# Attention as one written order over 40 units, with copies moved between ScalarE, VectorE and GpSimd

## The chip, the cores and the metric

The kernel runs on one core of a Trainium2 chip. The core has five engines that work side by side, each through its own instructions in order: TensorE (PE in the profile, matmuls, with PEld for its weight loads), VectorE (DVE), ScalarE (ACT), GpSimd (POOL) and SyncE (SP), which here issues nearly all DMA transfers. SBUF is the on-chip memory that all engines read; PSUM holds eight banks into which TensorE writes. The metric is the time of one execution on the device in microseconds (us); before the change it is 1604.54, the median of three runs (1601.63 to 1610.67).

## What is computed

A decoder block over 1024 tokens of width 1024, in float32. After a norm, one projection gives the inputs of two branches and of two gates: a state-space branch (branch a), and an attention branch with 8 heads of width 64 (branch b). The gated branches are merged, a feed-forward layer follows. The change concerns the attention:

```python
def one_block(args):
    qb, t0 = args
    z = jnp.einsum('bhqd,bhkd->bhqk', qb, kh) * scale
    q_pos = t0 + jnp.arange(Q_BLOCK, dtype=jnp.int32)[:, None]
    mask = key_pos < q_pos
    log_not = jnp.where(mask, jax.nn.log_sigmoid(-z), 0.0)
    suffix = lax.cumsum(log_not, axis=3, reverse=True) - log_not
    weights = jnp.where(mask, jnp.exp(jax.nn.log_sigmoid(z) + suffix), 0.0)
    return jnp.einsum('bhqk,bhkd->bhqd', weights, vh)
```

For every query a weight on each earlier key is needed, and it depends on a running sum over all keys between that key and the query. So the sums of one block of keys are carried on to the next block, from late keys to early ones.

## The kernel before

Heads are taken in four pairs (hp), the 1024 queries in two halves of 512 (Q). A pair and a half form a group. Within a group the keys are walked from late to early in blocks of 128 (kb). One step of this walk is a unit: two small blocks at once in the first step of a group, one block in the others. A group with Q=0 has three units, one with Q=1 has seven, so there are ten units per pair of heads and 40 in all. A unit covers 512 queries for two heads (tiles of 128 x 2 x 512) in 24 of the 40, and 384 in the 16 that lie on the diagonal and are cut by the mask.

A unit has three parts.

- `scores` (from L681): TensorE multiplies keys and queries into `z` in PSUM (L694). `z` is copied to SBUF as `wa`, with the mask added on the diagonal (L702, VectorE) or without (L704, VectorE). ScalarE computes abs, exp and log into `ws` (L705 to L707), VectorE completes the logarithm (L708). For the running sum in high precision, `ws` is split into a high part `wh` (L709, a cast on ScalarE) and the rest `wl` (L710, VectorE).
- the sums (L727 to L748): TensorE multiplies both parts by a triangle of ones into `acc` in PSUM (L731, L734), of which there is one buffer of two banks (the pool `accp`). Row 0 of it, added to the row so far, is the sum over all later keys (L740, L742, VectorE). It is written to DRAM (`cD`, L744) and read back spread over all 128 partitions as `wb` (L746), both issued by SP. The next unit subtracts that `wb` from its `wa` on GpSimd (L727) and its own `acc` on VectorE (L748). ScalarE takes the exponential (L749).
- the values (L753): TensorE multiplies the weights in `wa` by V into one PSUM bank per group, which ScalarE copies out at the group's end (L754).

Beside this runs work that does not depend on the attention and fills TensorE. It is 14 projection jobs: the queries and keys of head pairs 1 to 3 (`qk_proj`, six jobs) and the eight blocks of the second gate (`gate` with g=1). A job loads one weight block of 512 KB, splits it into a high and a low part (L411 on ScalarE or L413 on GpSimd, L414), and then issues two halves of 24 matmuls (L610) of 128 x 512 each. A half writes one PSUM bank, which is copied out by ScalarE (L647, L662) or VectorE (L645, L664). The pool for it, `mm`, has a single bank here, since the eight banks are shared out as one for `mm`, one for the values, four for `z` (two buffers) and two for `acc`. A gate block is then stored to DRAM (`gD`).

The order is not written by hand. A planner that simulates the kernel in time while it is built lays out each engine's instructions, first the ready ones, by their place in the program. The kernel influences it by edges that only order: `first=` in `qk_proj` and `gate` puts a weight load behind a chosen score matmul (`self.marks`, with `QPIN` and `PINS`). Behind the attention follows `branch_b`, which multiplies the outputs by w_b (L882) and applies the gates from DRAM.

Of the kernel before, what the change touches and what calls it, by code (L numbers as in the profile page):

```python
# [333 lines left out]
P = 128  # L334
KT = 8
# [37 lines left out]
class Turns:  # L373
# [5 lines left out]
    def tile(self, shape, dtype, name=None):  # L379
        pool, tag, *bufs = self.pools[self.n % len(self.pools)]  # L380
        self.n += 1
        return pool.tile(shape, dtype, name=tag, bufs=bufs[0] if bufs else None)


class Block:
# [295 lines left out]
    def scores(self, q, k, Q, kbs, work):  # L681


        nc = self.nc
        a, s = (work.tile([P, 2, 512], F32, name=t, bufs=b) for t, b in (("wa", WAB2), ("ws", WSB)))
        hi, lo = (work.tile([P, 2, 512], F32R, name=t, bufs=WHB) for t in ("wh", "wl"))
        z = self.zp.tile([P, 2, 512], F32, name="z")
        segs, f, prev, diag = [], 0, None, kbs[0] >= 4 * Q
        for kb in kbs:
            c = max(kb - 4 * Q, 0) * P  # L690
            w = 512 - c
            for x in range(2):
                h = slice(64 * x, 64 * x + 64)
                prev = nc.tensor.matmul(z[:, x, f:f + w], lhsT=k[h, P * kb:P * kb + P], rhs=q[h, 512 * Q + c:512 * Q + 512],  # L694
                                        start=True, stop=True)
            segs.append((kb, slice(f, f + w), slice(c, 512)))
            f += w
        self.marks.append(prev)
        at, st, ht, lt, z = (t[:, :, 0:f] for t in (a, s, hi, lo, z))
        if diag:  # L700
            m = P * (2 - len(kbs))
            nc.vector.tensor_tensor(at, z, self.mask[:, m:m + f].unsqueeze(1).broadcast_to([P, 2, f]), ALU.add)  # L702
        else:
            nc.vector.tensor_copy(at, z)  # L704
        nc.scalar.activation(st, at if diag else z, AF.Abs)  # L705
        nc.scalar.activation(st, st, AF.Exp, scale=-1.0)
        nc.scalar.activation(st, st, AF.Ln, bias=1.0)  # L707
        nc.vector.scalar_tensor_tensor(st, at, 0.0, st, ALU.max, ALU.add)  # L708
        nc.scalar.copy(ht, st)  # L709
        nc.vector.tensor_tensor(lt, st, ht.bitcast(F32), ALU.subtract)  # L710
        return a, (hi, lo), segs, f

    def heads(self, hp, q, k, V, work, out):


        nc = self.nc
        for Q in range(2):
            kbs = [(4 * Q + 3, 4 * Q + 2), (4 * Q + 1,), (4 * Q,)] + [(kb,) for kb in reversed(range(4 * Q))]
            av = self.avp.tile([P, 512], F32, name="mm")
            row = behind = None  # L720
            for unit in kbs:
                a, parts, segs, f = self.scores(q, k, Q, unit, work)
                kb, fs, c = segs[-1]
                if behind is not None:
                    old = slice(c.start + P if kb >= 4 * Q else 0, 512)
                    o = slice(old.start - c.start, 512 - c.start)
                    nc.gpsimd.tensor_tensor(a[:, :, o], a[:, :, o], behind[:, :, old], ALU.subtract)  # L727
                r = self.accp.tile([P, 2, 512], F32, name="acc")
                for x in range(2):
                    for n in range(2):  # L730
                        nc.tensor.matmul(r[:, x, 0:f], lhsT=self.upto, rhs=parts[n][:, x, 0:f], start=n == 0, stop=n == 1 and behind is not None)  # L731
                    if behind is None:
                        for n in range(2):
                            nc.tensor.matmul(r[:, x, f - P:f], lhsT=self.ones_r, rhs=parts[n][:, x, 0:P], start=False, stop=n == 1)  # L734
                if kb:
                    past, row = row, work.tile([P, 2, 512], F32, name="row", bufs=RWB)[0:1]
                    if c.start:
                        nc.gpsimd.memset(row[:, :, 0:c.start], 0.0)
                    if past is None:
                        nc.vector.tensor_copy(row[:, :, c], r[0:1, :, fs])  # L740
                    else:
                        nc.vector.tensor_tensor(row[:, :, c], past[:, :, c], r[0:1, :, fs], ALU.add)  # L742
                    d = self.cD[hp, Q, kb:kb + 1]
                    nc.sync.dma_start(out=d, in_=row.rearrange("p a b -> p (a b)"))  # L744
                    behind = work.tile([P, 2, 512], F32, name="wb", bufs=CBB)
                    nc.sync.dma_start(out=behind.rearrange("p a b -> p (a b)"), in_=d[0].partition_broadcast(P))  # L746
                for x in range(2):
                    nc.vector.tensor_tensor(a[:, x, 0:f], a[:, x, 0:f], r[:, x, 0:f], ALU.subtract)  # L748
                self.last_exp = nc.scalar.activation(a[:, :, 0:f], a[:, :, 0:f], AF.Exp)  # L749
                for kb, fs, c in segs:  # L750
                    for x in range(2):
                        h = slice(64 * x, 64 * x + 64)
                        nc.tensor.matmul(av[h, c], lhsT=V[:, kb, h], rhs=a[:, x, fs], start=kb == 4 * Q + 3, stop=kb == 0, skip_group_check=True)  # L753
            nc.scalar.copy(out[:, 512 * Q:512 * Q + 512], av)  # L754


    def ada_rest(self, ap, first):
# [423 lines left out]
    def run(self):  # L1181
        tc, nc, i = self.tc, self.nc, self.i
        with ExitStack() as es:
# [14 lines left out]
            w = (wp, "wh", "wl", wp, "ws", 2)  # L1198
# [3 lines left out]
            with ExitStack() as s1:  # L1202
                mm = s1.enter_context(self.pool("mm", 1, PSUM))
# [4 lines left out]
                gp = gps.enter_context(self.pool("g", GB, side="right"))  # L1208
# [12 lines left out]
                with ExitStack() as s3:  # L1221
                    with self.pool("ta", 2, side="right") as tp, \
# [12 lines left out]
                    vp = s3.enter_context(self.pool("v", 2))  # L1235
                    op = s3.enter_context(self.pool("o", 4))
                    with self.pool("tri", 1) as tri, self.pool("work", 1) as work, self.pool("zp", ZPB, PSUM) as self.zp, self.pool("acc", 1, PSUM) as self.accp:
                        self.avp = mg_
                        self.triangles(tri)
                        self.marks = []  # L1240
                        self.mm = mm
                        ops = []
                        for hp in range(4):
                            V = vp.tile([P, KT, P], F32, name="V")
                            nc.sync.dma_start(out=V, in_=self.vD.rearrange("(t p) d -> p t d", p=P)[:, :, P * hp:P * hp + P])
                            if hp:
                                qk.append(self.qk_proj(hp, qp, kp, self.marks[QPIN]))
                            q, k = qk[hp]
                            ops.append(op.tile([P, 1024], F32, name="o"))
                            self.heads(hp, q, k, V, work, ops[hp])  # L1250
# [4 lines left out]
                        for m in range(KT):  # L1255
                            self.gate(1, m, gp, self.marks[PINS[m]] if m else None, self.wring[2])
# [10 lines left out]
            with ExitStack() as s4:  # L1267
# [4 lines left out]
                wb = (self.W, "wb", "wb", wp, "ws", 2)  # L1272
# [43 lines left out]
```

## Time and profile before

| what | value |
|---|---|
| median of the runs | 1604.54 us |
| profiled execution, its own time | 1602.23 us |
| span of the profiled execution | 1600.5 us |
| busy: TensorE, VectorE, GpSimd, ScalarE | 1437.2, 1143.1, 783.8, 632.5 us |
| first score matmul to last value matmul | 409.4 to 728.5 us into the span |

A profile is one execution. Its time is a little longer than its span, from the first instruction to the last. Sums over parts of the span are therefore set against 1602.23 and not against the median. In a list in order of time, the first number of a line is the start, the second how long it lasted; matmuls overlap, so the pace of TensorE is read from starts. `x4` joins four instructions. A float32 matmul appears as two records. A bracket at a line's end gives how long the engine stood idle before it, and what released it. In groups of instructions the numbers behind the bar are the busy time in us, the mean in ns of one, and the idle time before them by releaser.

### The profile page before, as it was taken

How to read it: one execution, taken by the hardware profiler on the slowest of the kernel's cores; microseconds unless marked ns; L12 is line 12 of the kernel's file. 1: busy time of each engine (PE TensorE's matmuls, PEld its weight loads, DVE VectorE, ACT ScalarE, POOL GpSimd, SP SyncE). 2: the span in 40 equal slices, each digit the busy share in tenths (PEclk: the TensorE clock that was granted, in tenths of full speed). 3: DMA queues.
4: the chain of work that ended last, by engine and by line, in shares of the span. 5: the costliest groups of instructions: out<-in, count | busy, mean ns of one | idle time of the engine just before them, and what ended most of it. 6: DMA issues, size and time to landing. Idle time of an engine off the chain costs nothing.

```text
span 1600.5 us, 18352 instructions
## 1 busy us (share of the span) xinstructions
PE 1437.2 (90%) x6514; PEld 1125.3 (70%) x6514; DVE 1143.1 (71%) x1408; ACT 632.5 (40%) x812; POOL 783.8 (49%) x602
## 2 busy tenths in 40 slices
PE   4898889899878799989999879999999998999965
PEld 3688667778645365567778668888888887787854
DVE  6989777452577887663733796656666659999978
ACT  4421111452566776743314643223233324343313
POOL 3459774010332424341420445455554468889774
PEclk9999999899999899999999989999999999999988
DMA  9586656635321324235443413333333246445302
GB/s 240 168 197 176 175 145 187 180 103 168 103 79 67 119 86 150 80 110 195 145 158 111 131 48 99 112 111 115 115 113 108 66 159 247 148 148 165 100 26 105
DMA packets 195811, 210.45 MB, mean 131 GB/s; under 512 B 28612, under 2 KB 142376, under 8 KB 195720
## 3 DMA queue, kind: packets, MB, share of 16 engines
q1 hardware_dynamic: 184648, 201.29, 40.5%
q10 hardware_dynamic: 11072, 8.00, 1.7%
q8 instruction: 51, 0.84, 0.2%
q14 instruction: 40, 0.33, 0.1%
HBM read 159.18 MB, written 48.89 MB: 130 GB/s over the span
## 4 chain that ended last, share of the span: by engine, by line
PE 45%; DVE 21%; DMA 11%; issue 9%; POOL 8%; ACT 5%; SPq 0%; ACTq 0%; DVEq 0%; POOLq 0%
PE tq L1037 10%; PE wo L1037 8%; PE mm L610 7%; PE wo L918 5%; PE gu L1037 3%; DMA aw<-in_w_ada_dram 3%; PE tq L1119 2%; PE ga L610 2%; DVE acc L550 2%; PE wo L1119 1%; PE acc L731 1%; DVE acc L770 1%; DMA wb<-cD 1%; DVE f L1112 1%; PE z L694 1%
## 5 line engine op out<-in xcount | busy, mean ns | idle before, releaser
L727 POOL TENSOR_TENSOR wa<-wa,wb 128x1024 f32<-128x1024 f32 (+2 forms) x32 | 67.4, 2107 | 161.8 <-DMA wb<-cD 120.5
L430 POOL TENSOR_TENSOR ws<-wb 128x1024 f32<-128x1024 f32 x29 | 73.2, 2524 | 102.2 <-DVE wl L433 58.4
L430 POOL TENSOR_TENSOR wgs<-wb 128x1024 f32<-128x1024 f32 x15 | 37.9, 2526 | 109.8 <-DVE x L433 39.7
L708 DVE SCALAR_TENSOR_TENSOR ws<-wa,ws 128x1024 f32<-128x1024 f32 (+1 forms) x40 | 57.9, 1452 | 32.7 <-ACT ws L707 32.7
L610 PE MATMUL mm<-pb,wh 128*128 128x512 f32 x192 | 64.0, 414 | 6.8 <-DVE gst L645 4.1
L1090 POOL TENSOR_TENSOR pa<-pa,row 128x1024 f32<-128x1024 f32 x22 | 66.0, 3023 | 1.6 <-DMA pa<-in_w_ffn_down_dram 1.6
L748 DVE TENSOR_TENSOR wa<-wa,acc 128x512 f32<-128x512 f32 (+1 forms) x80 | 46.6, 620 | 23.3 <-POOL wa L727 23.3
L770 DVE SCALAR_TENSOR_TENSOR acc<-aw,cond,acc 128x512 f32<-128x512 f32 x56 | 51.9, 927 | 15.7 <-DMA aw<-in_w_ada_dram 15.1
L610 PE MATMUL mm<-pa,wh 128*128 128x512 f32 x192 | 62.4, 404 | 0.1
L1028 POOL TENSOR_TENSOR f<-f,f 128x512 f32<-128x512 f32 x30 | 49.1, 1662 | 26.0 <-DVE f L1018 17.5
L610 PE MATMUL mm<-pa,wgh 128*128 128x512 f32 x176 | 57.3, 407 | 4.3 <-POOL wgh L413 3.8
L411 ACT CAST wh<-ws 128x1024 fp32r<-128x1024 f32 x30 | 31.3, 1045 | 74.8 <-PE wo L918 32.5
L694 PE MATMUL z<-q,k 64*128 64x512 f32 (+3 forms) x192 | 47.3, 567 | 14.7 <-ACT ws L705 9.0
L610 PE MATMUL mm<-pb,wgh 128*128 128x512 f32 x176 | 56.7, 403 | 1.9 <-ACT gst L647 1.9
L414 POOL TENSOR_TENSOR wl<-ws,wh 128x1024 fp32r<-128x1024 f32 x10 | 27.4, 2739 | 62.2 <-ACT wh L411 62.2
L749 ACT ACTIVATE wa<-wa 128x1024 f32<-128x1024 f32 (+1 forms) x40 | 38.8, 969 | 46.6 <-DVE wa L748 46.6
L709 ACT CAST wh<-ws 128x1024 fp32r<-128x1024 f32 (+1 forms) x40 | 38.4, 961 | 40.5 <-DVE ws L708 35.8
L413 POOL TENSOR_SCALAR wgh<-wgs 128x1024 fp32r<-128x1024 f32 x8 | 11.3, 1417 | 87.2 <-DMA ws<-in_w_in_dram 59.2
L710 DVE TENSOR_TENSOR wl<-ws,wh 128x1024 fp32r<-128x1024 f32 (+1 forms) x40 | 52.0, 1302 | 2.1 <-ACT wh L709 2.0
L610 PEld LDWEIGHTS mm<-pb,wh 128*128 128x128 f32 x192 | 37.2, 198 | 19.7 <-DVE gst L645 4.5
L1110 POOL TENSOR_TENSOR wb<-pa 128x512 f32<-128x512 f32 x23 | 40.2, 1755 | 15.7 <-DVE wxl L1108 5.5
L1017 ACT ACTIVATE f<-f 128x1024 f32<-128x1024 f32 x22 | 23.3, 1061 | 56.5 <-DVE f L1057 29.1
(748 smaller groups left out, 4867.2 us busy)
## 6 DMA issues: line engine op xcount, KB each, us to landing
aw<-in_w_ada_dram SPq DMA_DIRECT2D x32, 512.0 KB
wb<-cD SPq DMA_DIRECT2D x32, 512.0 KB
hD<-f SPq DMA_DIRECT2D x30, 512.0 KB
wb<-in_w_ffn_gate_dram SPq DMA_DIRECT2D x44, 256.0 KB
wb<-in_w_ffn_up_dram SPq DMA_DIRECT2D x44, 256.0 KB
pa<-in_w_ffn_down_dram SPq DMA_DIRECT2D x22, 512.0 KB
wb<-hD SPq DMA_DIRECT2D x40, 256.0 KB
ws<-in_w_in_dram SPq DMA_DIRECT2D x19, 512.0 KB
```

The lines of the kernel that those rows point to most:

```text
L430: (add or nc.gpsimd).tensor_tensor(st, a, b, op)
L610: self.nc.tensor.matmul(ps, lhsT=w[a][:, k], rhs=act[h][k][:, b], start=(j == 0), stop=(j == n - 1))
L694: prev = nc.tensor.matmul(z[:, x, f:f + w], lhsT=k[h, P * kb:P * kb + P], rhs=q[h, 512 * Q + c:512 * Q + 512], start=True, stop=True)
L708: nc.vector.scalar_tensor_tensor(st, at, 0.0, st, ALU.max, ALU.add)
L710: nc.vector.tensor_tensor(lt, st, ht.bitcast(F32), ALU.subtract)
L727: nc.gpsimd.tensor_tensor(a[:, :, o], a[:, :, o], behind[:, :, old], ALU.subtract)
L770: nc.vector.scalar_tensor_tensor(acc, w[:, j], cj, acc, ALU.mult, ALU.add)
L918: nc.tensor.matmul(ps, lhsT=mg[t // 4][k][:, a, P * (t % 4):P * (t % 4) + P], rhs=ws[k // 2][b][:, k % 2], start=(j == 0), stop=(j == 23))
L1028: nc.gpsimd.tensor_tensor(o, a, b, op)
L1037: self.nc.tensor.matmul(ps, lhsT=w[x][:, q, k], rhs=self.B[i](y, k), start=(j == 0), stop=(j == 11))
L1090: nc.gpsimd.tensor_tensor(w, w, g2, ALU.mult)
L1119: nc.tensor.matmul(ps, lhsT=o[x][:, P * t:P * t + P], rhs=o[y][:, R], start=(j == 0), stop=(j == 3 * np_ - 1))
```

## The change

The functions `heads` and part of `scores` are replaced by one loop over all 40 units. `scores`, `sums` and `values` are now called for different units in one turn: the sums of unit i, the values of unit i-1, and the scores of unit i+3. The 14 projection jobs become a generator, `fillers`, that gives out one matmul at a time; 8 of them are issued behind the sums and 8 behind the scores of each turn, and 12 behind each of the first three scores. What is left comes at the end. Every TensorE instruction of this part goes through `pinned`, which ties it behind the one traced before it on that engine. The order of all other engines is still the planner's.

Beside the order these things change. The copy of a score without a mask (L704) goes from VectorE to ScalarE, and the abs that follows reads that copy in place of `z`. The high part (L709) goes from ScalarE to GpSimd, as a multiplication by one with float32 rounded on output, the operation of L413. `wa` has five buffers in place of four, `wb` one in place of two. The weights of a job are loaded two jobs ahead and take turns over the rings 0, 0 and 2, where queries and keys had ring 0 and the gate had ring 2 alone. All 28 halves of the jobs lie inside the loop; before, the last three halves of the gate ran behind the attention. The edges by `marks` are gone.

```diff
-WAB2, WSB, WHB, RWB, CBB = 4, 2, 2, 2, 2
+WAB2, WSB, WHB, RWB, CBB = 5, 2, 2, 2, 1
-QPIN = -10
-PINS = (0, 5, 10, 15, 20, 25, 30, 35)
+LOOK = 3
+FILL = (8, 8, 12)
+JOBS = (("q", 1), ("k", 1), ("g", 0), ("g", 1), ("q", 2), ("k", 2), ("g", 2), ("q", 3), ("k", 3), ("g", 3), ("g", 4), ("g", 5), ("g", 6), ("g", 7))
+AHEAD = 2
...
+    def pinned(self, *args, **kw):
+        return self.tc.keep_in_program_order(self.nc.tensor.matmul(*args, **kw))
+
+    def fillers(self, qk, qp, kp, gp):
+        nc = self.nc
+        rings = [self.wring[0], self.wring[0], self.wring[2]]
+        jobs = [(n, i) for n, i in JOBS]
+        loaded = []
+        def load(j):
+            n, i = jobs[j]
+            c0 = {"q": 512, "k": 1024, "g": 3072}[n] + P * i
+            loaded.append(self.w3(self.weight(self.in_cols(c0), lo_eng=nc.gpsimd, hi_eng=nc.gpsimd if n == "g" else None, ring=rings[j % 3])))
+        for j in range(AHEAD):
+            load(j)
+        for j, (n, i) in enumerate(jobs):
+            if j + AHEAD < len(jobs):
+                load(j + AHEAD)
...
+            for h in range(2):
+                s = slice(512 * h, 512 * h + 512)
+                ps = self.mm.tile([P, 512], F32, name="mm")
+                c = 0
+                for k in range(KT):
+                    for a, b in PRODUCTS:
+                        self.pinned(ps, lhsT=loaded[j][a][:, k], rhs=self.hT[h][k][:, b], start=c == 0, stop=c == 23)
+                        c += 1
+                        if c == 24:
+                            if n == "q":
+                                nc.scalar.activation(t[:, s], ps, AF.Copy, scale=0.125)
+                            elif n == "k":
+                                nc.vector.tensor_copy(t[:, s], ps)
+                            else:
+                                st = gp.tile([P, 512], F32, name="gst")
+                                (nc.vector.tensor_copy if h else nc.scalar.copy)(st, ps)
+                                nc.sync.dma_start(out=self.gD[1, P * i:P * i + P, s], in_=st)
+                        yield
...
         else:
-            nc.vector.tensor_copy(at, z)
-        nc.scalar.activation(st, at if diag else z, AF.Abs)
+            nc.scalar.copy(a, z)
+        nc.scalar.activation(st, a, AF.Abs)
...
-        nc.scalar.copy(ht, st)
+        nc.gpsimd.tensor_scalar(ht, st, 1.0, 0.0, ALU.mult, ALU.add)
...
+        for i in range(-LOOK, len(units) + 1):
+            if 0 <= i < len(units):
+                self.sums(units[i], work)
+                some(FILL[0])
+            if i > 0:
+                u = units[i - 1]
...
+                self.values(u, ops[u.hp])
+            if i + LOOK < len(units):
+                self.scores(units[i + LOOK], qk, work)
+                some(FILL[1] if i >= 0 else FILL[2])
+        some(10000)
+        return ops
```

`sums` and `values` hold the lines of the old `heads` (L727 to L749, and L753 with L754), with their matmuls pinned; `some(n)` takes n matmuls from `fillers`.

More of the change, by code (lines that the diff above doesn't have):

```diff
@@ L687, in scores @@
+    def scores(self, u, qk, work):
+        nc = self.nc
+        q, k = qk[u.hp]
+        u.a, s = (work.tile([P, 2, 512], F32, name=t, bufs=b) for t, b in (("wa", WAB2), ("ws", WSB)))
+        u.parts = [work.tile([P, 2, 512], F32R, name=t, bufs=WHB) for t in ("wh", "wl")]
         z = self.zp.tile([P, 2, 512], F32, name="z")
-        segs, f, prev, diag = [], 0, None, kbs[0] >= 4 * Q
-        for kb in kbs:
-            c = max(kb - 4 * Q, 0) * P
+        u.segs, f, diag = [], 0, u.kbs[0] >= 4 * u.Q
+        for kb in u.kbs:
+            c = max(kb - 4 * u.Q, 0) * P
@@ L713, in heads @@
-    def heads(self, hp, q, k, V, work, out):
-        nc = self.nc
[L717 to L754, printed above, removed]
@@ new lines, in sums @@
+    def sums(self, u, work):
+        nc, g, a, f = self.nc, u.group, u.a, u.f
+        kb, fs, c = u.segs[-1]
+        if g.behind is not None:
+            old = slice(c.start + P if kb >= 4 * u.Q else 0, 512)
+            o = slice(old.start - c.start, 512 - c.start)
+            nc.gpsimd.tensor_tensor(a[:, :, o], a[:, :, o], g.behind[:, :, old], ALU.subtract)
+        r = self.accp.tile([P, 2, 512], F32, name="acc")
+        for x in range(2):
+            for n in range(2):
+                self.pinned(r[:, x, 0:f], lhsT=self.upto, rhs=u.parts[n][:, x, 0:f], start=n == 0, stop=n == 1 and g.behind is not None)
+            if g.behind is None:
+                for n in range(2):
+                    self.pinned(r[:, x, f - P:f], lhsT=self.ones_r, rhs=u.parts[n][:, x, 0:P], start=False, stop=n == 1)
+        if kb:
+            past, g.row = g.row, work.tile([P, 2, 512], F32, name="row", bufs=RWB)[0:1]
+            if c.start:
+                nc.gpsimd.memset(g.row[:, :, 0:c.start], 0.0)
+            if past is None:
+                nc.vector.tensor_copy(g.row[:, :, c], r[0:1, :, fs])
+            else:
+                nc.vector.tensor_tensor(g.row[:, :, c], past[:, :, c], r[0:1, :, fs], ALU.add)
+            d = self.cD[u.hp, u.Q, kb:kb + 1]
+            nc.sync.dma_start(out=d, in_=g.row.rearrange("p a b -> p (a b)"))
+            g.behind = work.tile([P, 2, 512], F32, name="wb", bufs=CBB)
+            nc.sync.dma_start(out=g.behind.rearrange("p a b -> p (a b)"), in_=d[0].partition_broadcast(P))
+        for x in range(2):
+            nc.vector.tensor_tensor(a[:, x, 0:f], a[:, x, 0:f], r[:, x, 0:f], ALU.subtract)
+        self.last_exp = nc.scalar.activation(a[:, :, 0:f], a[:, :, 0:f], AF.Exp)
@@ new lines, in values, with attention, some @@
+    def values(self, u, out):
+        g = u.group
+        for kb, fs, c in u.segs:
+            for x in range(2):
+                h = slice(64 * x, 64 * x + 64)
+                self.pinned(g.av[h, c], lhsT=g.V[:, kb, h], rhs=u.a[:, x, fs], start=kb == 4 * u.Q + 3, stop=kb == 0, skip_group_check=True)
+        if kb == 0:
+            self.nc.scalar.copy(out[:, 512 * u.Q:512 * u.Q + 512], g.av)
+    def attention(self, qk, qp, kp, vp, op, gp, work):
+        nc = self.nc
+        units, ops = [], []
+        for hp in range(4):
+            for Q in range(2):
+                g = Bag(behind=None, row=None, av=None, V=None)
+                for kbs in [(4 * Q + 3, 4 * Q + 2), (4 * Q + 1,), (4 * Q,)] + [(kb,) for kb in reversed(range(4 * Q))]:
+                    units.append(Bag(hp=hp, Q=Q, kbs=kbs, group=g))
+        fill = self.fillers(qk, qp, kp, gp)
+        def some(n):
+            for _ in range(n):
+                next(fill, None)
+        V = None
+        for i in range(-LOOK, len(units) + 1):
[4 more added lines that the diff above has]
+                u = units[i - 1]
+                if u.group.av is None:
+                    if u.Q == 0:
+                        V = vp.tile([P, KT, P], F32, name="V")
+                        nc.sync.dma_start(out=V, in_=self.vD.rearrange("(t p) d -> p t d", p=P)[:, :, P * u.hp:P * u.hp + P])
+                        ops.append(op.tile([P, 1024], F32, name="o"))
+                    u.group.V = V
+                    u.group.av = self.avp.tile([P, 512], F32, name="mm")
+                self.values(u, ops[u.hp])
[4 more added lines that the diff above has]
+        return ops
@@ L1239, in run @@
                         self.triangles(tri)
-                        self.marks = []
                         self.mm = mm
[L1242 to L1250, printed above, removed]
+                        qk = [list(qk[0])] + [[None, None] for _ in range(3)]
+                        ops = self.attention(qk, qp, kp, vp, op, gp, work)
                         spare = []
```

27 lines of the change are left out of this document (13 added, 14 removed).

## The prediction

> **What bounds the kernel now.** I read the engines' shares first, then the stretch in which the attention runs, cut out of the trace from its first score matmul to its last value matmul, and what follows up to the end of the projection behind it.
>
> ```profile
> PE 1437.2 (90%) x6514; PEld 1125.3 (70%) x6514; DVE 1143.1 (71%) x1408; ACT 632.5 (40%) x812; POOL 783.8 (49%) x602
> 409.40:728.50 319.10, 281.27 (x1178) 173.57 (x1178) 232.77 (x246) 207.91 (x230) 120.30 (x67) 0.95 0.30 96
> 728.50:797.10 68.60, 65.96 (x300) 54.61 (x298) 41.66 (x49) 26.91 (x41) 21.91 (x12) 0.98 0.55 184
> ```
>
> The first number after a window is its length, then TensorE, weight loads, VectorE, ScalarE and GpSimd. TensorE is the busiest engine overall and in this stretch too, but here it idles 319.1 - 281.3 = 37.8 us, while the stretch behind is full. What TensorE must do there at full speed I take from spacings of matmuls, in order of time; the first column is the start. S are the sums (L731, L734), V the values (L753), Z the scores (L694), L610 the projections that fill in.
>
> ```profile
> 500.01 0.44 PE L731 MATMUL acc<-wh,upto 128*128 128x384 f32 x1
> 501.30 1.08 PE L753 MATMUL mm<-wa,V 128*64 128x512 f32 x4
> 507.65 0.33 PE L731 MATMUL acc<-wh,upto 128*128 128x384 f32 x1
> 508.44 0.87 PE L753 MATMUL mm<-wa,V 128*64 128x128 f32 x8
> 509.24 1.13 PE L694 MATMUL z<-q,k 64*128 64x512 f32 x4
> 510.30 0.49 PE L610 MATMUL mm<-pb,wl 128*128 128x512 f32 x1
> 565.76 0.93 PE L694 MATMUL z<-q,k 64*128 64x128 f32 x8
> 566.62 1.08 PE L753 MATMUL mm<-wa,V 128*64 128x512 f32 x4
> 708.46 1.08 PE L753 MATMUL mm<-wa,V 128*64 128x512 f32 x4
> 709.47 0.73 PE L610 MATMUL mm<-pb,wgh 128*128 128x512 f32 x2
> 715.05 0.39 PE L731 MATMUL acc<-wh,upto 128*128 128x512 f32 x1
> 716.05 1.08 PE L753 MATMUL mm<-wa,V 128*64 128x512 f32 x4
> ```
>
> A full unit (512 queries, 24 of the 40) takes S 716.05 - 715.05 = 1.00, V 709.47 - 708.46 = 1.01, Z 510.30 - 509.24 = 1.06, together 3.07. The 16 narrower ones take Z 0.86 and V 0.80, with S 1.29 where a group begins (8) and 0.79 else (8). Sum: 24 x 3.07 + 8 x 2.95 + 8 x 2.45 = 116.9 us. Half a projection job, 24 matmuls, takes 715.05 - 709.47 = 5.58, or 0.2325 each. Of 28 halves 25 lie in the stretch and three (16.7 us) behind it, among the second branch's projection. So the stretch holds 116.9 + 25 x 5.58 = 256.4 us of work and takes 319.1: 62.7 us are lost, some 38 idle and some 25 by matmuls at a lower clock. Why it idles, the waits say (waiting line, releaser, us, times, longest):
>
> ```profile
> POOL wa L727 <- DMA wb<-cD: 120.5, 26, 14.0
> ...
> PEld acc L731 <- DVE wa L748: 13.3, 7, 4.0
> ...
> PE acc L731 <- DVE wa L748: 11.1, 8, 3.3
> ```
>
> S of a unit waits until L748 has read the one S buffer, L748 for L727 on GpSimd, and L727 for a row that goes through DRAM. The other waits are scores behind a late ScalarE and projections behind late weights.
>
> **The change part by part.** *The written order.* Each turn of the new loop issues on TensorE S(i), 8 fills, V(i-1), Z(i+3), 8 fills; three turns before it issue Z and 12 fills. All 14 jobs, 28 halves, now lie in it: floor 116.9 + 28 x 5.58 = 273.1 us, against 319.1 + 16.7 = 335.8 for the same work before. The most to be gained is 62.7. From that go five costs.
>
> *(1) The hand-over of the projection's bank.* The fills write one PSUM bank, and the copy out of it must end before the next half starts. After the 36 warm-up matmuls the blocks are 8 long, and a half ends at multiples of 24: 36 + 8n is never such a multiple after 24, so 26 of 27 hand-overs fall four matmuls into a block, with nothing of TensorE in between. Before, other work usually stood there (715.05 above). Where it did not:
>
> ```profile
> 757.10 0.39 PE L610 MATMUL mm<-pb,wgl 128*128 128x512 f32 x1
> 758.27 0.73 PE L882 MATMUL mm<-V,wh 128*128 128x512 f32 x2 [0.78 <-DVE gst L645]
> 420.96 0.33 PE L731 MATMUL acc<-wh,upto 128*128 128x384 f32 x1
> 424.86 0.84 PE L610 MATMUL mm<-pb,wh 128*128 128x512 f32 x2 [2.66 <-ACT q L662]
> 428.50 0.74 PE L610 MATMUL mm<-pb,wh 128*128 128x512 f32 x2
> ```
>
> With VectorE free TensorE resumes 758.27 - 757.33 (one spacing after 757.10) = 0.94 later; with ScalarE's queue full (the half ends where S begins at 420.96), 424.86 - 420.96 = 3.90 later, 2.66 of it idle. Bounds 26 x 0.94 = 24.4 and 26 x 3.90 = 101. I take the low end plus what is left of an operation under way: by the engine sums below ScalarE and VectorE are some 60% busy with operations of about 1.1 us, so 0.6 x 0.55 = 0.35 more. 26 x 1.3 = 33.8 us. This is the largest and least certain term.
>
> *(2) The start.* Z is now pinned behind fills whose weights are not there.
>
> ```profile
> 409.38 1.57 PE L694 MATMUL z<-q,k 64*128 64x128 f32 x12 [1.66 <-DVE gst L851]
> 413.29 0.73 PE L610 MATMUL mm<-pa,wh 128*128 128x512 f32 x2
> 415.80 0.50 PE L610 MATMUL mm<-pa,wl 128*128 128x512 f32 x1
> ```
>
> After Z(0) (0.86, to 410.3) the first fill waits to 413.3 and the third, on the low part, to 415.8: 3.0 + 2.0 = 5.0 less what stood before, taken as 4.9; nothing if the weights come sooner.
>
> *(3) GpSimd and the row through DRAM.* The chain of waits shows one round with free engines:
>
> ```profile
> 718.65 3.81 DMA wb<-cD
> 722.59 2.40 POOL wa L727
> 725.02 1.29 DVE wa L748 x2
> ```
>
> With one wb buffer instead of two, the next wb load also waits for L727: 722.59 - 718.65 + 2.40 = 6.34 us a round, below TensorE's pace of 3.07 + 16 x 0.2325 + 0.65 x 1.3 = 7.64 a full unit (0.65 hand-overs). On SP the waiting load has weight loads behind it, but those are issued two jobs, some 40 us, ahead. On GpSimd come the high parts:
>
> ```profile
> L710 DVE TENSOR_TENSOR wl<-ws,wh 128x1024 fp32r<-128x1024 f32 x24 | 36.9, 1538 | 1.1 <-ACT wh L709 1.0
> L704 DVE COPY wa<-z 128x1024 f32<-128x1024 f32 x16 | 19.4, 1210 | 0.0
> L414 POOL TENSOR_TENSOR wgl<-wgs,wgh 128x1024 fp32r<-128x1024 f32 x7 | 19.9, 2841 | 0.9 <-PE mm L610 0.5
> L413 POOL TENSOR_SCALAR wgh<-wgs 128x1024 fp32r<-128x1024 f32 x7 | 10.3, 1469 | 76.1 <-DMA ws<-in_w_in_dram 59.2 <-issue 16.9
> L709 ACT CAST wh<-ws 128x1024 fp32r<-128x1024 f32 (+1 forms) x40 | 38.4, 961 | 40.5 <-DVE ws L708 35.8
> L705 ACT ACTIVATE ws<-z 128x1024 f32<-128x1024 f32 x16 | 16.4, 1024 | 4.4 <-DVE wa L704 4.2
> ```
>
> L413 is the operation the high part becomes: 24 x 1.47 + 16 x 1.10 (three quarters as wide) = 52.9 us, 1.32 a unit; the weights' 14 low parts and 8 high parts are 1.31 a unit. Both fit the 3.94 between a wb load and L727: zero at the low end; at the high end all stand in the way and the round is 6.34 + 2.63 = 8.97, over the pace by 1.33 in 24 rounds, 32 us. I take 3, since the cover is there.
>
> A rule speaks against this move: the Trainium skill, SBUF — State Buffer, section on its two separate sides, says that a VectorE operation with two SBUF inputs and a GpSimd operation exclude each other for a whole instruction. The trace agrees:
>
> ```profile
> 692.13 2.41 POOL L727 TENSOR_TENSOR wa<-wa,wb 128x1024 f32<-128x1024 f32 x1 [2.03 <-DMA wb<-cD]
> 694.49 2.04 POOL L413 TENSOR_SCALAR wgh<-wgs 128x1024 fp32r<-128x1024 f32 x1
> 692.47 3.15 DVE L710 TENSOR_TENSOR wl<-ws,wh 128x1024 fp32r<-128x1024 f32 x1
> ```
>
> L710 started into L727 and ended 1.1 after it, and L413 took 2.04 by standing behind L710. By that rule a round could grow a further 1.0, to 9.97, and the time by 24 x 1.0 = 24 us.
>
> *(4) ScalarE and VectorE.* The copy of a score moves to ScalarE: 16.4 us more there (as L705 on z; the 1.02 stands in a unit's latency, hidden by three units, some 20 us, of lead), 19.4 less on VectorE; the 40 casts, 38.4, leave ScalarE. Stretch sums become 185.9, 213.4 and 177 (GpSimd), of some 320: no engine passes TensorE, and these moves are worth nothing directly.
>
> *(5) The end.* In the last three turns there is no Z and one block: 1.00 + 1.86 + 1.01 = 3.87 against the round of 6.34, so some 2.5 twice: 5 us (0 to 10 if hand-overs add). The copy and split of the last output are covered by the 20 fills left. Behind it the gates no longer cover the second branch's loads; it has eight banks to run ahead, so 2 us, between 0 and the landing of one load as long as wb's (3.81).
>
> Sum: 273.1 + 33.8 + 4.9 + 3 + 5 + 2 = 321.8, 14.0 below 335.8. The profiled execution took 1602.23 (span 1600.5); 1602.2 - 14.0 = 1588.2, and with the 2.3 by which the median 1604.54 lies above it, 1590.
>
> **The rivals.** *B, it runs as written:* hand-overs at 0.94, no cost in (3) and (5): 273.1 + 24.4 + 4.9 = 302.4, a gain of 33.4: 1571. For it: 120.5 us of GpSimd's idle time is wait for the wb load, so it has room. Against: both copying engines run over half the time.
>
> *C, the round through wb and GpSimd sets the pace:* 8.97 a round, 32 us instead of 3: 1619. For it: the single buffer, and L414 at 2.84 in front of L727. Against: 1.2 us spare a unit, and groups break the chain 8 times. It makes the kernel slower than the noise from a round of 8.7 on. With the exclusion of the two engines in every round as well, as the page has it, it would be 1643; the trace bears it out in single pairs, and I count it within C's chance.
>
> *D, slower, by the hand-overs alone:* the copy is queued behind score work on ScalarE or a waiting L748 on VectorE and costs the 2.66 of the row at 424.86 each: 26 x 2.66 = 69.2, 35.4 more than taken: 1626. It gives the whole gain back from 1.84 us a hand-over. For it: that row. Against: a written order can put the copy first. After 2.66 idle matmuls also ran slow: 9 in 428.50 - 424.86 = 3.64 us, 1.5 more than at 0.2325. The Trainium skill, TensorE: Matmul & The Clock Gate, Part 1, lowers the clock after an idle window of some 3.4 us, so by it D's gaps would cost nothing more; the trace has them slow already at 2.66, which would put D at 1666.
>
> *E, no change:* the S buffer is still single, and half of the 13.3 + 11.1 us that S waited for L748 stays, 12 instead of 3: 1599, within the noise. For it: nothing in the change shortens that path.
>
> **How the numbers follow.** The forecast 1590 gets 0.42, with its own range 1577 to 1602; B 0.16, E 0.13, C 0.13, D 0.16. A measurement of this kernel tells about 0.5%, 8 us, from no change: faster is below 1596.5. Four fifths of the forecast's chance and all of B: 0.50. A fifth of it and E: 0.21. C and D: 0.29. The range runs from a little under B to a little over D, 1558 to 1636.
>
> **What would show it.** In the new profile the first score to the last value should take about 315 us. TensorE's idle before L610-like fills should name the copies of q, k and the gates as releasers, some 26 times at about 1 us; waits of S for L748 should have shrunk from 24.4. If that stretch takes 340 or more, the releaser of the longest idle tells C (DMA wb, GpSimd) from D (the copies). If GpSimd's high parts take over 1.47, or VectorE's L710 over 1.54, the exclusion is dearer than taken. The prediction is wrong if the stretch shrinks but the next one grows by as much.

## The result, and the profile after

The changed kernel is slower: 1617.17 us, median of six runs (1613.79 to 1623.72), against 1603.57 for the kernel before in six runs. The ratio is 1.0092, with an interval of 1.0071 to 1.0112. The forecast was 1590, and faster; the time lies inside its range of 1558 to 1636, but the change went the other way. Medians and ratios below leave out one execution of 2821.12 us, of the run with the high part back on ScalarE, which is far off all others.

The same views as before, of the kernel after. In its code the line numbers have moved: the pinned matmuls all have L692, the copies out of the fills' bank are L724 (q), L726 (k) and L729 (gate), the high part is L761, the rest `wl` L762, the subtraction of `wb` L772, and that of the sums L793. L754 adds the mask to a score, L760 completes the logarithm, L787 adds up the row. First the two windows, from the first score to the last value and on to the end of the second branch's projection: length, then busy time of TensorE, weight loads, VectorE, ScalarE and GpSimd, then the granted clock, DMA share and GB/s.

```profile
408.40:755.50 347.10, 297.81 (x1231) 186.86 (x1231) 213.04 (x230) 189.96 (x205) 150.55 (x107) 0.93 0.26 88
755.50:809.20 53.70, 53.70 (x241) 44.85 (x240) 39.47 (x47) 25.86 (x39) 18.22 (x10) 0.94 0.63 213
```

Together they take 400.8 us against 387.7 before, 13.1 more; the spans differ by 12.5. So the whole loss is here, and it is in the first window: 347.1 against 319.1 plus the 16.7 of gate work that has moved into it. TensorE now idles 347.1 - 297.8 = 49.3 us there, where it idled 37.8. Who it waits for (waiting line, releaser, us, times, longest):

```profile
PE mm L692 <- DVE gst L729: 21.6, 7, 5.0
PE mm L692 <- DVE k L726: 10.5, 6, 2.7
PE mm L692 <- ACT gst L729: 6.7, 8, 1.0
PE acc L692 <- DVE wa L793: 5.6, 2, 4.8
PE mm L692 <- ACT q L724: 4.8, 5, 1.4
PE z L692 <- DVE gst L938: 1.7, 1, 1.7
```

The last row, for a copy of the first gate (L938), lies ahead of the window. Of the kernel before, beside the waits of the sums that the prediction shows:

```profile
PE z L694 <- ACT ws L705: 9.0, 6, 3.3
...
PE mm L610 <- POOL wgh L413: 3.8, 3, 1.6
...
PE mm L610 <- ACT q L662: 2.7, 1, 2.7
```

Those for a late score or late weights are gone, and those at the sums are down to two. In their place stand 26 waits for the copy out of the fills' single bank, 7 + 6 + 8 + 5, worth 43.6 us. The 13 copies on ScalarE cost 0.89 each, the 13 on VectorE 2.47. The dearest, in order of time, on TensorE, VectorE and GpSimd:

```profile
473.72 0.39 PE L692 MATMUL mm<-pb,wgl 128*128 128x512 f32 x1
479.09 1.22 PE L692 MATMUL mm<-pa,wh 128*128 128x512 f32 x2 [4.97 <-DVE gst L729]
480.10 0.63 PE L692 MATMUL mm<-pa,wl 128*128 128x512 f32 x1
484.80 0.72 PE L692 MATMUL mm<-pa,wh 128*128 128x512 f32 x2
485.36 0.40 PE L692 MATMUL mm<-pa,wl 128*128 128x512 f32 x1
```

```profile
472.41 1.20 DVE L787 TENSOR_TENSOR row<-row,acc 1x1024 f32<-1x1024 f32 x1
473.54 1.27 DVE L793 TENSOR_TENSOR wa<-wa,acc 128x512 f32<-128x512 f32 x2
474.73 1.21 DVE L760 SCALAR_TENSOR_TENSOR ws<-wa,ws 128x1024 f32<-128x1024 f32 x1
477.21 1.23 DVE L762 TENSOR_TENSOR wl<-ws,wh 128x1024 fp32r<-128x1024 f32 x1 [1.27 <-POOL wh L761]
478.35 0.68 DVE L729 COPY gst<-mm 128x512 f32<-128x512 f32 x1
```

```profile
476.13 1.05 POOL L761 TENSOR_SCALAR wh<-ws 128x1024 fp32r<-128x1024 f32 x1 [4.72 <-DVE ws L760]
```

The half ends at 474.1. Its copy takes 0.68 us, but on VectorE it is queued behind the subtraction of the sums, the logarithm's last step and the rest part, which in turn waits 1.27 for the high part on GpSimd. It starts at 478.35, and TensorE, whose order is fixed, has nothing else to issue. When it resumes, it is slow: 11 matmuls from 480.10 to 484.80, 0.427 us each, where 0.2325 is full speed. The granted clock, the third number from the end, is 0.50 in these 4.7 us:

```profile
480.10:484.80 4.70, 4.70 (x13) 3.62 (x12) 1.90 (x3) 0.83 (x1) 3.28 (x2) 0.50 0.13 48
```

That lost another 2.1 us.

The work in the window is 273.1 us at full speed, by the prediction's count. What is over that and over the idle time is matmuls at a lower clock, and the ends of matmul records that reach into a stall: 347.1 - 49.3 - 273.1 = 24.7 us. Before it was 335.8 - 37.8 - 273.1 = 24.9. The written order did not get rid of it.

### The profile page after: what moved, and what is told of

It reads as the page before. It is cut to its first block, busy times and chain, and to the rows that moved or that the text cites. A ratio compares the mean times of both kernels' runs of the same rounds, so it can differ in the third digit from the quotient of the medians.

```text
span 1613.0 us, 18318 instructions
## 1 busy us (share of the span) xinstructions
PE 1442.3 (89%) x6514; PEld 1131.0 (70%) x6514; DVE 1124.2 (70%) x1392; ACT 616.1 (38%) x788; POOL 819.9 (51%) x642
## 4 chain that ended last, share of the span: by engine, by line
PE 29%; DVE 10%; issue 5%; POOL 4%; DMA 2%; ACT 1%; POOLq 0%; DVEq 0%; ACTq 0%
PE tq L1124 11%; PE wo L1124 9%; PE wo L1005 5%; PE gu L1124 3%; POOL pa L1177 1%; DMA pa<-in_w_ffn_down_dram 1%; DVE x L1212 1%; POOL pb L1216 1%; POOL wb L1197 1%; DVE pb L1212 1%; DVE f L1199 1%; DVE wl L1195 1%; DVE f L1195 1%; DVE ft L439 1%; DVE ss L462 0%
## 5 line engine op out<-in xcount | busy, mean ns | idle before, releaser
L761 POOL TENSOR_SCALAR wh<-ws 128x1024 fp32r<-128x1024 f32 (+1 forms) x40 | 38.4, 961 | 126.1 <-DVE ws L760 88.3
L772 POOL TENSOR_TENSOR wa<-wa,wb 128x1024 f32<-128x1024 f32 (+2 forms) x32 | 67.5, 2110 | 57.2 <-DMA wb<-cD 49.5
L423 POOL TENSOR_TENSOR wl<-ws,wh 128x1024 fp32r<-128x1024 f32 x14 | 35.5, 2536 | 110.1 <-ACT wh L420 92.0
L692 PE MATMUL mm<-pa,wh 128*128 128x512 f32 x160 | 60.0, 450 | 22.1 <-DVE gst L729 18.2
L762 DVE TENSOR_TENSOR wl<-ws,wh 128x1024 fp32r<-128x1024 f32 (+1 forms) x40 | 52.0, 1299 | 33.0 <-POOL wh L761 32.9
L793 DVE TENSOR_TENSOR wa<-wa,acc 128x512 f32<-128x512 f32 (+1 forms) x80 | 46.7, 621 | 37.6 <-POOL wa L772 36.3
L794 ACT ACTIVATE wa<-wa 128x1024 f32<-128x1024 f32 (+1 forms) x40 | 38.8, 971 | 88.4 <-DVE wa L793 79.9
L692 PE MATMUL mm<-pb,wh 128*128 128x512 f32 x160 | 53.7, 408 | 9.4 <-ACT gst L729 5.1
L692 PEld LDWEIGHTS mm<-pa,wh 128*128 128x128 f32 x160 | 32.8, 216 | 38.1 <-DVE gst L729 20.8
L760 DVE SCALAR_TENSOR_TENSOR ws<-wa,ws 128x1024 f32<-128x1024 f32 (+1 forms) x40 | 51.9, 1298 | 10.1 <-ACT ws L759 10.0
L857 DVE SCALAR_TENSOR_TENSOR acc<-aw,cond,acc 128x512 f32<-128x512 f32 x56 | 47.0, 839 | 13.5 <-DMA aw<-in_w_ada_dram 12.8
L420 ACT CAST wh<-ws 128x1024 fp32r<-128x1024 f32 x28 | 29.3, 1048 | 68.6 <-PE wo L1005 32.9
L757 ACT ACTIVATE ws<-wa 128x1024 f32<-128x1024 f32 (+1 forms) x40 | 39.0, 975 | 42.9 <-DVE wa L754 42.2
L1197 POOL TENSOR_TENSOR wb<-pa 128x512 f32<-128x512 f32 x23 | 40.1, 1753 | 15.6 <-DVE wxl L1195 5.5
L787 DVE TENSOR_TENSOR row<-row,acc 1x1024 f32<-1x1024 f32 (+1 forms) x24 | 26.9, 1119 | 29.3 <-PE acc L692 29.2
L692 PEld LDWEIGHTS mm<-pb,wh 128*128 128x128 f32 x160 | 29.3, 189 | 25.5 <-ACT gst L729 7.9
L692 PE MATMUL z<-q,k 64*128 64x512 f32 (+3 forms) x192 | 43.2, 541 | 1.7 <-DVE gst L938 1.7
```

Source lines behind the costliest of these rows:

```text
L692: return self.tc.keep_in_program_order(self.nc.tensor.matmul(*args, **kw))
L760: nc.vector.scalar_tensor_tensor(st, a, 0.0, st, ALU.max, ALU.add)
L772: nc.gpsimd.tensor_tensor(a[:, :, o], a[:, :, o], g.behind[:, :, old], ALU.subtract)
L857: nc.vector.scalar_tensor_tensor(acc, w[:, j], cj, acc, ALU.mult, ALU.add)
L1197: nc.gpsimd.tensor_tensor(st[:, R], u, W[p][b[0]][:, 512 * b[1]:512 * b[1] + 512], SIGN_B[i])
```

## The experiments

Two theories were set against each other. H: the hand-over of the fills' bank, exposed in the middle of a block, is the loss. G: the high part on GpSimd holds up VectorE, and through it everything, and the late copies are only where it shows.

**Hand-overs at the ends of blocks.** One number of the changed kernel:

```diff
-FILL = (8, 8, 12)
+FILL = (8, 8, 8)
```

After 24 matmuls of warm-up, each half ends with the third block of 8, and values and scores, or sums, follow it. The 12 matmuls saved in front come at the end.

> The changed kernel with 8 fills in place of 12 behind each of the first three scores, so that every half of a job ends at the end of a block of 8 and the next matmuls are values and scores (2.07 us) or sums (1.00 us). Theory H (the single bank's hand-over, exposed in mid-block, is the loss): of the 43.6 us that TensorE stood there some 11 stay, the excess of the long ones over the cover, and some 10 us of lowered clock go too: 1570 to 1585, faster than the changed kernel by 2 to 3 per cent. Theory G (the high part on GpSimd holds up VectorE and with it everything): the wait moves to the sums, which wait for L793, and the time falls by 5 us at most: 1612.

Measured 1580.66 us; to the kernel before 0.9859 (0.9841 to 0.9876). Window of the attention, and TensorE's waits in it:

```profile
409.20:717.50 308.30, 282.20 (x1219) 177.07 (x1219) 218.16 (x230) 187.99 (x204) 152.98 (x107) 0.97 0.30 98
```

```profile
PE mm L692 <- ACT gst L729: 10.5, 6, 2.4
PE acc L692 <- DVE wa L793: 7.3, 4, 4.3
PE mm L692 <- ACT q L724: 3.2, 4, 1.7
PE mm L692 <- DVE k L726: 2.0, 2, 1.2
...
PE mm L692 <- DVE gst L729: 1.0, 2, 0.7
```

The waits for the bank fall from 43.6 to 16.7 us, those for VectorE's gate copies from 21.6 to 1.0. The window is 38.8 us shorter: 23.2 less idle, 15.6 less slow matmuls (308.3 - 26.1 - 273.1 = 9.1). H had it at 1570 to 1585, G at 1612.

**Three banks for the fills.** One z buffer in place of two frees two banks:

```diff
-ZPB = 2
+ZPB = 1
...
+ ..., self.pool("m2", 2, PSUM) as m2:
-                        self.mm = mm
+                        self.mm = Turns((mm, "mm"), (m2, "m2"), (m2, "m2"))
```

> The changed kernel with one buffer for z in place of two (two banks freed) and the fills taking turns over three banks in place of one. Theory H: no hand-over is exposed, 43.6 us of idle and most of the 20 us of lowered clock go: 1555 to 1580, if z's single buffer costs nothing, since a score has a whole turn to be copied out. Theory G: TensorE stops at the sums for L793 in their place, 1605 or more. If Z waits for its buffer, that shows as idle before the scores with the copy of z as releaser.

Measured 1575.10 us; 0.9823 (0.9807 to 0.9839), with the blocks of the changed kernel.

```profile
406.20:713.50 307.30, 281.55 (x1230) 178.35 (x1230) 217.30 (x230) 187.04 (x205) 152.52 (x107) 0.98 0.30 99
```

```profile
PE acc L692 <- DVE wa L793: 21.9, 17, 5.2
PE z L692 <- DVE wa L754: 1.7, 1, 1.7
```

No wait for a fill's copy is left, and z's single buffer costs 1.7 us. Now a second limit comes out that the hand-overs had covered: the sums wait 21.9 us for L793, 17 times. That is where G expected TensorE to stop, but the time is H's. So of the 43.6 us only half shows in the idle time (25.8 against 49.3), and the rest of the gain in the window is clock: 307.3 - 25.8 - 273.1 = 8.4 us of slow matmuls against 24.7.

**All copies out of the bank on ScalarE.**

```diff
-                                nc.vector.tensor_copy(t[:, s], ps)
+                                nc.scalar.copy(t[:, s], ps)
...
-                                (nc.vector.tensor_copy if h else nc.scalar.copy)(st, ps)
+                                nc.scalar.copy(st, ps)
```

> The changed kernel with all copies out of the fills' bank on ScalarE (those of k and of the second gate halves were on VectorE). Theory H: what matters is how late the copy is; the 13 that VectorE made cost TensorE 2.47 us each against 0.89 for the 13 of ScalarE, so 13 x 1.6 = 20 us go, and with a little clock the time is 1590 to 1597. Theory G: the copies were only where the delay showed; the sums wait in their place: 1610 to 1617.

Measured 1605.22 us; 1.0003 (0.9987 to 1.0020).

```profile
PE mm L692 <- ACT gst L729: 19.4, 15, 3.4
PE mm L692 <- ACT q L724: 10.5, 5, 4.0
PE mm L692 <- ACT k L726: 8.4, 6, 2.9
```

12 us faster than the changed kernel, but only half of what H expected. The 26 waits sum to 38.3 us, 1.47 each: the price of a hand-over belongs to the queue in front of the copy and not to the engine, and ScalarE's queue got longer. Both theories missed here; H by size.

**The high part back on ScalarE.**

```diff
-        nc.gpsimd.tensor_scalar(ht, st, 1.0, 0.0, ALU.mult, ALU.add)
+        nc.scalar.copy(ht, st)
```

> The changed kernel with the high part back on ScalarE (L761 a cast there), all else as changed. Theory G: VectorE no longer waits for GpSimd's high part (32.9 us) with the bank's copy behind it, the 13 hand-overs by VectorE fall from 2.47 to some 1.2 us: 1600 or below. Theory H alone: the hand-over is exposed all the same, VectorE's order is as full, and ScalarE's copies get later by the 38 us of casts on it: 1612 to 1620.

Measured 1615.91 us, the median of six executions; 1.0076 (1.0048 to 1.0105), which cannot be told from the changed kernel.

```profile
PE mm L692 <- DVE gst L729: 23.7, 7, 6.5
PE mm L692 <- DVE k L726: 11.1, 6, 3.0
```

```profile
L762 DVE TENSOR_TENSOR wl<-ws,wh 128x1024 fp32r<-128x1024 f32 x24 | 36.1, 1504 | 21.2 <-ACT wh L761 21.2
```

VectorE's rest part waits for ScalarE's high part instead, and its copies of the bank are as late: 34.8 us against 32.1. GpSimd is not what makes them late, so G falls.

**The moves alone, in the old order.** The kernel before, with the score copy on ScalarE and the high part on GpSimd:

```diff
-            nc.vector.tensor_copy(at, z)
-        nc.scalar.activation(st, at if diag else z, AF.Abs)
+            nc.scalar.copy(at, z)
+        nc.scalar.activation(st, at, AF.Abs)
...
-        nc.scalar.copy(ht, st)
+        nc.gpsimd.tensor_scalar(ht, st, 1.0, 0.0, ALU.mult, ALU.add)
```

> The kernel before, with the planner's order and its edges, and only the two moves: the unmasked score's copy on ScalarE (abs reads the copy) and the high part on GpSimd. Theory H (the loss is the written order's exposed hand-over): the moves are worth little in any order, 1597 to 1613. Theory G (GpSimd's high part is the harm): 1615 or more. A third, that the moves gain and the order took it away: 1590 or less.

Measured 1607.42 us; 1.0029 (1.0008 to 1.0051). The moves cost some 0.3 per cent and gain nothing, which H allowed and G and the third theory did not.

**The order alone.** The changed kernel with both moves undone:

```diff
-            nc.scalar.copy(a, z)
-        nc.scalar.activation(st, a, AF.Abs)
+            nc.vector.tensor_copy(a, z)
+        nc.scalar.activation(st, a if diag else z, AF.Abs)
...
-        nc.gpsimd.tensor_scalar(ht, st, 1.0, 0.0, ALU.mult, ALU.add)
+        nc.scalar.copy(ht, st)
```

> The changed kernel with both moves undone: only the written order, the five wa and the one wb buffer. Theory H: as the changed kernel, 1612 to 1625, with the hand-overs of the bank standing for 40 to 50 us of TensorE's idle. Theory G: 1605 or less.

Measured 1616.06 us; 1.0083 (1.0051 to 1.0114).

```profile
PE mm L692 <- DVE gst L729: 18.9, 7, 4.6
PE mm L692 <- DVE k L726: 12.5, 6, 4.2
PE mm L692 <- ACT gst L729: 8.2, 8, 1.8
...
PE mm L692 <- ACT q L724: 4.6, 5, 1.6
```

26 waits again, 44.2 us. The loss is there in full without the two moves. This run keeps the changed buffers of `wa` and `wb` and the changed rings of the weights, which were not undone by themselves; but the runs with aligned blocks and with three banks keep them too, and are faster than the kernel before.

**What holds the kernel with three banks.** Four edits looked at the 21.9 us at the sums. First, two wb buffers and four wa:

```diff
-WAB2, WSB, WHB, RWB, CBB = 5, 2, 2, 2, 1
+WAB2, WSB, WHB, RWB, CBB = 4, 2, 2, 2, 2
```

> The kernel with three banks for the fills, and besides four wa and two wb buffers in place of five and one. With the hand-over gone, TensorE stands 21.9 us at the sums for L793. If the single wb buffer sets that round, half of it goes: 1562 to 1568. If the round is set by the way of a row through DRAM and by GpSimd's queue, the time stays at 1572 to 1578; that a fifth wa is needed would show as scores' copies waiting for the values, and a longer time.

Measured 1578.15 us; 0.9828 (0.9799 to 0.9858). The sums still wait 23.1 us for L793, so a second wb buffer does not shorten the round. That the lost fifth `wa` hid a gain is unlikely: no copy of a score waits for the values in this trace.

Then more fills at the end, where no scores are left:

```diff
-FILL = (8, 8, 12)
+FILL = (8, 7, 12)
...
-                some(FILL[0])
+                some(FILL[0] + (14 if i >= len(units) - LOOK else 0))
```

> The kernel with three banks for the fills, with 7 fills in place of 8 behind the scores and the 37 so saved put into the last three turns (22 in place of 8 each), where no scores are left. The idle of 5.2 and 2.0 us at the last two sums, and the slow matmuls behind it, should go: 1566 to 1570. If the turns before get shorter by one fill and wait for L793 by as much, nothing is won: 1573 to 1577.

Measured 1574.44 us; 0.9812 (0.9787 to 0.9836). The window got shorter, 301.2 us against 307.3, but in this build the planner's order before it put the first score at 411.5 against 406.2, and the gain is gone. Over the twelve kernels, the ten of these experiments, the one before and the changed one, the first score lies between 402.8 and 412.6, though nothing was edited ahead of it. A difference of a few us between two kernels is therefore read from their windows and not from their medians.

Then the high part on ScalarE with three banks:

```diff
-        nc.gpsimd.tensor_scalar(ht, st, 1.0, 0.0, ALU.mult, ALU.add)
+        nc.scalar.copy(ht, st)
```

> The kernel with three banks for the fills, with the high part back on ScalarE. The hand-over no longer hides the round through wb and GpSimd: TensorE stands 21.9 us at the sums for L793, and L793 34.6 us for L772 on GpSimd. If GpSimd's load by the high part (38 us) makes L772 late, the time falls to 1562 to 1570; if VectorE gains nothing by it, it stays at 1572 to 1578; if ScalarE's casts come late behind the other score work, 1580 or more.

Measured 1571.12 us; 0.9819 (0.9767 to 0.9870), inside the interval of the three banks alone. The window is 305.9 us against 307.3, and the first score comes at 402.8 against 406.2, which is most of the difference. The sums still wait 20.7 us, so the high part on GpSimd is not what holds them either. What stands in front of L793 here:

```profile
POOL wa L772 <- DMA wb<-cD: 146.1, 27, 11.2
DVE wa L793 <- POOL wa L772: 35.8, 21, 4.9
```

GpSimd has time to spare and waits for the row through DRAM; VectorE waits for GpSimd. In 6 of the 15 waits at the sums of over 0.4 us, though, VectorE came to L793 straight from other work. Which of the two sets the round no edit has shown.

Last, without the extra banks, aligned blocks and, for one z buffer, two buffers for the sums:

```diff
-ZPB = 2
+ZPB = 1
-FILL = (8, 8, 12)
+FILL = (8, 8, 8)
...
-self.pool("acc", 1, PSUM) as self.accp
+self.pool("acc", 2, PSUM) as self.accp
```

> The changed kernel with hand-overs at the ends of blocks (8 fills in place of 12 behind the first three scores) and, with one z buffer, two buffers of two banks for the sums in place of one; the fills keep one bank. The sums need no longer wait for L793 of the unit before: of the 27.7 us of idle that the kernel with aligned hand-overs has, the 7.3 for L793 go, 1570 to 1575. If the fills' copies are what is left, 1577 to 1582.

Measured 1583.54 us; 0.9883 (0.9839 to 0.9928). This is just above both expectations. The waits for L793 at the sums are gone, but those for the fills' bank rise from 16.7 to 20.7 us, and 2.9 are new at the sums for L762: the turns are no shorter (a window of 308.3 us in both kernels), TensorE waits at the next place. What would take both away was not tried; eight banks hold three for fills or two pairs for sums, not both.

## Why the prediction was wrong

**What bounds the kernel: right.** The loss was where it was sought, TensorE's window in the attention, with 62.7 us to be gained. The count of work, 273.1 us, is borne out by the kernel with three banks: 307.3 us, of which 25.8 idle, leaves 281.5, only 8.4 above it.

**Step (1), the hand-over: the right place and number, the wrong size.** It named 26 exposed hand-overs; there are 26. It took 1.3 us for each, 0.94 plus a third of one operation under way, 33.8 in all. They took 43.6 us of idle and, since a stalled matmul's record reaches 0.39 - 0.23 = 0.16 into the stall, 1.84 each, 47.8 in all. That is just the figure at which rival D was said to give the whole gain back. This step failed. The failing assumption is that the copy comes next once its engine is free. On ScalarE it nearly did (0.89 idle). On VectorE up to four operations stood in front of it, in 10 of the 13 cases L762, which itself had waited for its high part, and 2.47 was the mean. Rival D took 2.66 idle for each from the row at 424.86; in that gap sums stood too, so that the bank there came free 3.90 us after the half's end, and the two figures lie close partly by chance. Rival D, with a chance of 0.16, is nearest to what happened: its mechanism, in full on one of the two copying engines. The prediction's own test says so as well: the stretch took 347.1 us, over its mark of 340, and the longest idle, 4.97 us, ended with a copy of the bank.

**A term that the sum put at nothing: the clock.** The prediction had the price of it, 1.5 us behind a stall of 2.66, and wrote it only into D. Its own sum has no slow matmuls at all, that is, it counted all 24.9 us of them as gained. In the changed kernel 24.7 remained, 26 x 0.16 = 4.2 of them the record ends that the 47.8 hold already, so 20.5 on their own. With aligned blocks 9.1 are left and with three banks 8.4: most of it comes from the hand-overs. This is the larger miss, 20.5 us against 14.0 on the hand-overs themselves.

**Step (2), the start: wrong, in the kernel's favour.** The first fills' weights come sooner than before: their load is issued at 388.95 where it was 400.75, the first high part is cast at 397.26 where it was 412.21, and the fills do not wait. Whether it is the missing edge that let the planner issue the load earlier was not tried. Of the kernel before:

```profile
400.75 1.07 SPq L404 DMA_DIRECT2D ws<-in_w_in_dram x2
412.21 1.03 ACT L411 CAST wh<-ws 128x1024 fp32r<-128x1024 f32 x1
```

Of the kernel after:

```profile
388.95 0.38 SPq L413 DMA_DIRECT2D ws<-in_w_in_dram x1
397.26 1.05 ACT L420 CAST wh<-ws 128x1024 fp32r<-128x1024 f32 x1
408.44 0.93 PE L692 MATMUL z<-q,k 64*128 64x128 f32 x8 [1.74 <-DVE gst L938]
409.30 0.75 PE L692 MATMUL mm<-pa,wh 128*128 128x512 f32 x2
409.88 0.60 PE L692 MATMUL mm<-pa,wl 128*128 128x512 f32 x1
```

The 4.9 us were not lost. With step (3) below, the terms balance: 321.8 predicted, less 4.9 for the start and 3 for the round, plus 14.0 for the hand-overs (47.8 for 33.8) and 24.7 - 4.2 = 20.5 of slow matmuls, is 348.4. Measured are 400.8 for both windows less 51.9 of the second one's own work, 348.9. This is bookkeeping and no proof, since the 24.7 is what the first window has left over; that both terms belong to the hand-overs is shown by the runs without them.

**Step (3), GpSimd and the row through DRAM: right in this kernel.** The sums wait for L793 only twice, 5.6 us, both among the last turns. GpSimd's high part is cheaper than L413 had it:

```profile
L761 POOL TENSOR_SCALAR wh<-ws 128x1024 fp32r<-128x1024 f32 x24 | 25.1, 1047 | 101.8 <-DVE ws L760 64.9 <-PE mm L692 23.5 <-PE z L692 8.7
L762 DVE TENSOR_TENSOR wl<-ws,wh 128x1024 fp32r<-128x1024 f32 x24 | 35.9, 1495 | 23.7 <-POOL wh L761 23.7
```

1.05 us, not 1.47, and none of the 24 took longer than that. The likely reason is its place: it comes between two VectorE operations of one chain, L760 and L762, and L762 cannot start before it. The rest part, at 1.50, is no slower than before (1.54). The exclusion of the two engines is in this trace too:

```profile
469.01 2.40 POOL L772 TENSOR_TENSOR wa<-wa,wb 128x1024 f32<-128x1024 f32 x1
```

```profile
469.07 3.41 DVE L762 TENSOR_TENSOR wl<-ws,wh 128x1024 fp32r<-128x1024 f32 x1 [1.27 <-POOL wh L761]
```

L762 ends 1.07 us after L772, about its own length, as the Trainium skill has it (SBUF — State Buffer, the section on its two separate sides). But with the high part on ScalarE L762 takes 1.50 as well, so it is not this move that makes it long. Rival C, that this round sets the pace, did not hold here. Something like it shows once the hand-overs are gone, with 21.9 us at the sums, but a second wb buffer left it at 23.1 and a GpSimd without the high part at 20.7; its cause stays open.

**Step (4), the moves: right.** Alone they make 1.0029, and undone 1.0083 against 1.0092.

**Step (5), the end: right.** The last two sums wait 0.8 and 4.8 us, 5.6 for 5 predicted. The second branch took 53.7 us where 68.6 - 16.7 = 51.9 was its own work, 1.8 for 2 predicted.

**Rival B**, that it runs as written, said 1571. With three banks the kernel takes 1575.10: that is what the written order is worth when the bank is not in its way, 1.8 per cent to the good. That it comes near B's figure is chance, since B had 24.4 us of hand-overs in it and this kernel has none, but waits at the sums and slow matmuls in their place.

## What to carry to other kernels

A written order on one engine is only as good as the slowest hand-over inside it: where two neighbours in the order share a buffer, count at which position of the pattern the buffer changes hands, and put other work there or give it another buffer. Here 36 or 24 matmuls of warm-up ahead of the blocks of 8 decided over 36 us. Price such a hand-over by the queue in front of the copying engine, not by the copy, and add what the clock takes behind a stall.

## What the runs showed of the hardware

In seven of these kernels, the one before, the changed one and five of the experiments, I set the length of each stall of TensorE in the attention, from 0.6 us on, against the pace of the fills right behind it (mean spacing of eight of them, without the matmul that resumes). Below 1.6 us the pace stayed at 0.23 to 0.27 us a matmul in 89 of 96 stalls; three of the other seven came 4.4 us behind a stall of over 3.5. Between 1.6 and 3.6 us it was above 0.27 in 32 of 48, and went either way: in the changed kernel 0.23 after 1.73 us and 0.30 after 1.94, where the first of them came 0.43 apart. Above 3.6 us it was 0.31 to 0.45 in all 16, for some five us, as behind the row at 479.09. The Trainium skill, TensorE: Matmul & The Clock Gate, Part 1, names an idle window of some 3.4 us for this; the runs agree above it, but the clock also fell after less than 2 us of idle (0.61 granted from 557 to 561, right behind that stall of 1.94). A stall of 2 us can so cost 4, which an engine's idle time does not show.
